# The opening of a two-layer backbone: modulation in quarters on four column tiles, the values of five row pairs summed side by side, in a hand-written order

## The chip, the cores and the metric

The kernel runs on one core of a Trainium2 chip, in one launch. Its engines are TensorE (PE in the profile, with its weight loads as PEld), VectorE (DVE), ScalarE (ACT), GpSimd (POOL) and SyncE (SP), which here does nothing but issue transfers. SBUF is the on-chip memory, PSUM the eight banks into which TensorE sums (128 partitions, 512 fp32 numbers per partition and bank). The metric is the device time of one execution in microseconds, the median over several runs.

## What is computed

A backbone of two layers over 1024 latent tokens and 256 context tokens of width 1024. Layer 0 is windowed attention with sink logits, layer 1 latent attention. The change touches only what comes first in layer 0: the modulation of the normalised tokens, and the projection onto the values.

```python
def adaln(cond, w, bias):
    m = jax.nn.silu(cond) @ w + bias
    return jnp.split(m, 3, axis=-1)          # shift, scale, gate

shift_x, scale_x, gate_x = adaln(c, ada_w[i], ada_b[i])
shift_c, scale_c, gate_c = adaln(c_ctx, ada_w[i], ada_b[i])
hx = rms_norm(x, norm_g[i]) * (1.0 + scale_x[:, None]) + shift_x[:, None]
hc = rms_norm(ctx, norm_g[i]) * (1.0 + scale_c) + shift_c
...
q, k, v, g = jnp.split(h @ w_in, [A_WIDTH, A_WIDTH + A_KV_WIDTH, A_WIDTH + 2 * A_KV_WIDTH], axis=-1)
```

Here `ada_w[0]` is 1024 x 3072 in fp32; its first 2048 columns (shift and scale) are 8 MB. The value columns of `w_in` are 256 wide.

## The kernel before, in words

**Tiling.** The 1280 tokens are ten row tiles of 128, in five pairs `p`: pair 0 is the context, pairs 1 to 4 the latent tokens. The width of 1024 is eight blocks `k` of 128 columns, taken in four quarters `b` of two blocks. A group is one pair and one quarter; there are 20.

**The opening** is everything until the first projection of the loop `proj_t`. For each row tile it loads the tile (`x_load`), sums its squares on ACT (`norm`, L692), takes the root on POOL (L693, L694) and scales the tile in place (`scale`, L701 on DVE, L699 on ACT). For each group it turns four 128 x 128 blocks on TensorE into a PSUM bank (`turn`, L712), multiplies and adds the modulation's columns on DVE (`h_part`, two instructions at L723), and cuts the result into a high part, rounded on ACT (L724), and the low remainder, a subtraction on POOL or DVE (`h_low`, L729). `v_part` then sums the values: for two blocks and two row tiles three matmuls each, high x high, low x high and high x low (`mm3`, L126, L127, L128), so 12 matmuls of 128 x 256 for each group. After a pair's fourth quarter ACT and DVE take the values out of PSUM (L745, L747).

**The modulation.** The columns of shift and scale come from `ada_mm`: the 1024 rows of `ada_w` pass as moving data in eight pieces `k`, with two columns of conditioning (latent, context) as weights, in two halves `h` of 512 shift and 512 scale columns. The shift's two rows land in PSUM partitions 0 and 1, the scale's in 32 and 33, of bank 6. `ada_cols` copies them out on ACT (L679), turns them into columns on TensorE (L681), and `set_cols` adds bias and gain on DVE (L168, L171). No `h_part` of quarters 0 and 1 can start before half 0 is complete, none of quarters 2 and 3 before half 1.

**Buffers.** `arena_f` holds staging in fp32: six pieces of `ada_w`, four row tiles, two pieces of the value weights and four group buffers. With four places for row tiles, pairs 0 and 1 run through all their quarters first, half 0 and then half 1, and pairs 2 to 4 follow. Four PSUM banks take the turned groups, two the values of a pair in turn.

**What sets the order.** In the opening the order on each engine is found by the scheduler of the language from the program's order and its own reckoning of readiness. From the loop on (`in_order = tc.manual_schedule()`) the program's order stands. All loads of the opening are issued by SP, which works through them in order; a load waits for the buffer it overwrites, and also for the transfer issued eight before it among all queues, since eight semaphores tell of landings in turn. Queues of the other engines are worked through in order as well.

**After the opening** come the projections of the first layer (ten column blocks of `w_in`, blocks 1 to 9 in the loop), with a vector computation of the remaining modulation beside them on DVE (`ada_vec`, L342 and L344).

## Time and profile before

| | us |
|---|---|
| median of 3 runs (1560.34 to 1561.45) | 1561.43 |
| the profiled execution, its own time | 1563.35 |
| its span, first to last instruction | 1561.6 |
| PE busy in the span | 1513.9 |
| DVE, ACT, POOL busy | 953.2, 714.1, 816.3 |
| HBM read and written | 131.13 MB, 46.15 MB |

The profiled execution's own time lies 1.75 us above its span, and 1.9 us above the median. In the page each line of the span in slices gives ten per cent steps of busy time for 40 equal slices of 39 us; the opening fills a little more than the first two of them, where PE reads 6 and 8 while it reads 9 nearly everywhere else.

### The profile page before, as it was taken

How to read it: one execution, taken by the hardware profiler on the slowest of the kernel's cores; microseconds unless marked ns; L12 is line 12 of the kernel's file. 1: busy time of each engine (PE TensorE's matmuls, PEld its weight loads, DVE VectorE, ACT ScalarE, POOL GpSimd, SP SyncE). 2: the span in 40 equal slices, each digit the busy share in tenths (PEclk: the TensorE clock that was granted, in tenths of full speed). 3: DMA queues.
4: the chain of work that ended last, by engine and by line, in shares of the span. 5: the costliest groups of instructions: out<-in, count | busy, mean ns of one | idle time of the engine just before them, and what ended most of it. 6: DMA issues, size and time to landing. Idle time of an engine off the chain costs nothing.

```text
span 1561.6 us, 24793 instructions
## 1 busy us (share of the span) xinstructions
PE 1513.9 (97%) x9074; PEld 1207.1 (77%) x9074; DVE 953.2 (61%) x1859; ACT 714.1 (46%) x1369; POOL 816.3 (52%) x764
## 2 busy tenths in 40 slices
PE   6899999999999999998999999999999999999998
PEld 2797888687888888887988788766876875885686
DVE  2666968827767787777826301556566566566644
ACT  2512212219877777776623332244443443453422
POOL 2652545417544443344517351278789789699200
PEclk8899999999999999999999999999999999999999
DMA  8425544474433322326304851402122112211442
GB/s 303 178 92 186 198 140 169 151 223 138 121 109 99 97 89 88 95 68 203 109 9 138 295 155 63 124 9 58 45 68 65 51 46 74 58 44 45 142 155 81
DMA packets 123986, 178.91 MB, mean 115 GB/s; under 512 B 11724, under 2 KB 72268, under 8 KB 123864
## 3 DMA queue, kind: packets, MB, share of 16 engines
q1 hardware_dynamic: 119032, 170.27, 34.8%
q10 hardware_dynamic: 4832, 7.06, 1.3%
q8 instruction: 71, 1.16, 0.3%
q14 instruction: 51, 0.42, 0.1%
HBM read 131.13 MB, written 46.15 MB: 114 GB/s over the span
## 4 chain that ended last, share of the span: by engine, by line
PE 86%; DMA 3%; DVE 3%; ACT 3%; issue 2%; POOL 2%; SPq 0%; POOLq 0%; DVEq 0%; ACTq 0%
PE PB L126 14%; PE PB L127 14%; PE PB L128 14%; PE PB L1345 12%; PE PB L1368 9%; PE PB L572 5%; PE PB L1311 5%; PE PB L562 4%; PE PB L532 2%; PE PB L533 2%; DMA arena_f<-a_w_in 1%; PE PB L1379 1%; DVE arena_f L344 1%; DMA arena_f<-b_w_in 1%; PE PB L355 1%
## 5 line engine op out<-in xcount | busy, mean ns | idle before, releaser
L126 PE MATMUL PB<-arena_r 128*128 128x512 f32 (+2 forms) x1312 | 477.2, 364 | 4.9 <-ACT arena_r L205 2.1
L127 PE MATMUL PB<-arena_r 128*128 128x512 f32 (+2 forms) x1312 | 470.0, 358 | 2.9 <-POOL arena_r L729 2.0
L128 PE MATMUL PB<-arena_r 128*128 128x512 f32 (+2 forms) x1312 | 469.8, 358 | 0.2 <-DVE arena_r L122 0.2
L126 PEld LDWEIGHTS PB<-arena_r 128*128 128x128 f32 x1312 | 250.6, 191 | 58.9 <-issue 16.0
L1361 POOL TENSOR_TENSOR arena_f<-arena_f 128x1024 f32<-128x1024 f32 x120 | 285.9, 2382 | 8.2
L127 PEld LDWEIGHTS PB<-arena_r 128*128 128x128 f32 x1312 | 250.4, 191 | 37.3 <-POOL arena_r L729 2.6
L128 PEld LDWEIGHTS PB<-arena_r 128*128 128x128 f32 x1312 | 250.2, 191 | 35.6 <-DVE arena_r L122 0.4
L1345 PE MATMUL PB<-arena_r 64*128 64x512 f32 (+1 forms) x1600 | 225.8, 395 | 0.0
L122 POOL TENSOR_TENSOR arena_r<-arena_f,arena_r 128x512 fp32r<-128x512 f32 x98 | 134.7, 1388 | 164.4 <-ACT arena_r L121 164.3
L1317 DVE TENSOR_REDUCE krF<-PB 128x1 f32<-128x512 f32 (+1 forms) x264 | 167.3, 678 | 79.6 <-PE PB L1311 79.6
L1355 ACT ACTIVATE arena_f<-PB 128x1024 f32<-128x1024 f32 x160 | 164.5, 1028 | 111.4 <-PE PB L1345 84.6
L122 DVE TENSOR_TENSOR arena_r<-PB,arena_r 128x512 fp32r<-128x512 f32 (+2 forms) x215 | 140.4, 664 | 92.4 <-ACT arena_r L121 91.5
L1345 PEld LDWEIGHTS PB<-arena_r 64*128 64x128 f32 (+1 forms) x1600 | 174.0, 185 | 17.2 <-issue 5.2
L121 ACT CAST arena_r<-PB 128x512 fp32r<-128x512 f32 (+2 forms) x215 | 120.4, 565 | 120.6 <-PE PB L128 74.0
L539 DVE CUSTOM_DVE_ANT_0 arena_f<-PB,arena_f,small 128x256 f32<-128x256 f32 (+1 forms) x288 | 145.4, 524 | 46.1 <-PE PB L533 39.4
L1368 PE MATMUL PB<-arena_f 128*64 128x512 f32 x640 | 145.9, 595 | 0.0
L545 ACT ACTIVATE arena_f<-arena_f,small 128x640 f32<-128x640 f32 (+2 forms) x160 | 118.9, 744 | 28.8 <-DVE small L539 27.9
L572 PE MATMUL PB<-arena_r 128*128 128x512 f32 x336 | 120.7, 435 | 4.2 <-ACT arena_f L583 4.1
L344 DVE SCALAR_TENSOR_TENSOR arena_f<-arena_f,small 128x512 f32<-128x512 f32 x98 | 112.9, 1198 | 11.6 <-DMA arena_f<-ada_w 11.3
L1311 PE MATMUL PB<-arena_r 64*128 64x512 f32 (+1 forms) x768 | 109.5, 354 | 0.7 <-DVE arena_r L122 0.7
L1368 PEld LDWEIGHTS PB<-arena_f 128*64 128x64 f32 x640 | 44.0, 137 | 79.6 <-issue 79.0
L562 PE MATMUL PB<-ident,arena_f 128*128 128x128 f32 x672 | 104.8, 273 | 0.5 <-ACT arena_f L545 0.3
(165 smaller groups left out, 1869.6 us busy)
## 6 DMA issues: line engine op xcount, KB each, us to landing
arena_r<-q_d SPq DMA_DIRECT2D x160, 128.0 KB, 3.0
arena_f<-ada_w SPq DMA_DIRECT2D x64, 256.0 KB, 3.6
arena_f<-a_w_in SPq DMA_DIRECT2D x40, 256.0 KB, 3.8
arena_f<-ada_w SPq DMA_DIRECT2D x16, 512.0 KB, 5.0
arena_f<-x SPq DMA_DIRECT2D x16, 512.0 KB, 6.3
q_d<-arena_f SPq DMA_DIRECT2D x16, 512.0 KB, 2.6
qn_d<-arena_f SPq DMA_DIRECT2D x16, 512.0 KB, 5.1
arena_r<-qn_d SPq DMA_DIRECT2D x16, 512.0 KB
```

Source lines behind the costliest of these rows:

```text
L122: (lo_eng or nc.vector).tensor_sub(lo, src, hi.bitcast(F32))
L126: nc.tensor.matmul(o, ah, bh, start=first, stop=False)
L127: nc.tensor.matmul(o, al, bh, start=False, stop=False)
L128: nc.tensor.matmul(o, ah, bl, start=False, stop=last)
L562: nc.tensor.transpose(pt[:, h, :], self.Ps[h][:, ci * 128 : ci * 128 + 128], ident)
L572: nc.tensor.matmul(self.pv, V[:, self.chunks[ci], self.g, :], PT[:, s], start=ci == 0 and s == 0, stop=ci == self.m - 1 and s == 1,)
L1311: nc.tensor.matmul(bank[:, o : o + n], self.q[r, s, bs], k[r, 0, n0 : n0 + n], start=s == 0, stop=s == 2)
L1317: nc.vector.reduce_max(self.mxp[:, e, b : b + 1, i], bank[:, 0:n], AX.X)
L1345: nc.tensor.matmul(PB[:, b + e, :], k[r, s, cs], q[r, sq], start=i == 0, stop=i == 4)
L1355: nc.scalar.activation(E, PB[:, b : b + 2, :], AF.Exp)
L1361: eng.tensor_add(acc, acc, E)
L1368: nc.tensor.matmul(PB[r, 7, :], Vq[:, c, h, :], E[:, e], start=c == 0, stop=c == NT - 1)
```

## The change

The opening is written anew, and its order is now the program's (a second `manual_schedule`).

- **Modulation in quarters.** `ada_load(q, kk)` loads two blocks of rows and 256 shift and 256 scale columns, in two transfers of 256 KB (32 transfers in place of 16 of 512 KB). `ada_mm(q, kk)` issues four matmuls of 256 columns into PSUM partitions 0, 32, 64 and 96: the even and the odd block are summed apart. `ada_cols` adds the two while it turns them, by a matmul with a selecting matrix `sel`. Each quarter of the modulation releases one quarter of the groups. The number of columns that pass through TensorE is the same.
- **All row tiles stay.** Ten places for row tiles, each with an address of its own; `ada_w` has four staging places.
- **Values of all pairs in five banks.** Bank `p` sums pair `p` over all quarters, so the groups can run quarter by quarter. That leaves banks 5 and 7 for turned groups (two in place of four) and two group buffers in place of four.
- **Order of a group's matmuls.** `v_part` issues its eight matmuls with the high part first, and then the four with the low part.
- **Smaller moves.** The mean and epsilon step goes from POOL to DVE for a pair at once, the root for a pair in one instruction; squares are written to PSUM or to `V` as scratch; three of the high parts and one weight cut are rounded on POOL.

```diff
+    awr = Ring(F, [0, 10, 14, 18], 1024)
+    hr = Ring(F, [62, 64], 512)
...
+    def ada_load(q, kk):
+        aw[q, kk] = shp(awr.next(), 2, 2, 256)
+        src = t["ada_w"][0, kk * 256 : kk * 256 + 256, 0 : 2 * D].rearrange("(k p) (a c) -> p k a c", p=128, a=2)
         for a in range(2):
-            nc.tensor.matmul(PA[32 * a : 32 * a + 2], sc[:, k, :], aw[h, k][:, a, :], start=k == 0, stop=k == 7)
+            load(out=aw[q, kk][:, :, a], in_=src[:, :, a, q * 256 : q * 256 + 256])
+
+    def ada_mm(q, kk):
+        for k in range(2):
+            for a in range(2):
+                r = 64 * k + 32 * a
+                nc.tensor.matmul(
+                    PA[r : r + 2, 0:256], sc[:, 2 * kk + k, :], aw[q, kk][:, k, a], start=kk == 0, stop=kk == 3
+                )
+
+    def ada_cols(q):
+        for j in range(2):
+            o = PA[:, 256 + 34 * j : 290 + 34 * j]
+            nc.tensor.matmul(o, am[0:98, j * 128 : j * 128 + 128], sel[0:98], start=True, stop=True)
...
+    def x_load(p):
+        xn[p] = [f_at(22 + 8 * p, 2, 1024), sm_ring(), sm_ring()]
...
+    def norm(p):
+        _, sq, st = xn[p]
+        nc.vector.tensor_scalar(st[:, 0:2], sq[:, 0:2], 1.0 / D, EPS, ALU.mult, ALU.add)
+        nc.gpsimd.tensor_tensor(st[:, 2:4], st[:, 0:2], mhalf.to_broadcast([128, 2]), ALU.pow)
...
             for k in (2 * b, 2 * b + 1):
-                mm3(o, [h[:, s, k, js] for s in range(2)], [W[:, s, k, :] for s in range(2)], k == j == 0, j == 1 and k == 7)
+                for s in range(2):
+                    nc.tensor.matmul(o, h[:, 0, k, js], W[:, s, k, :], start=k == j == s == 0, stop=False)
+        for j in range(2):
+            js = slice(j * 128, j * 128 + 128)
+            o = PB[:, p, j * 256 : j * 256 + 256]
+            for k in (2 * b, 2 * b + 1):
+                nc.tensor.matmul(o, h[:, 1, k, js], W[:, 0, k, :], start=False, stop=j == 1 and k == 7)
...
+    groups = [(p, q) for q in range(2) for p in range(3)] + [(3, 0), (3, 1), (4, 0), (4, 1)]
+    groups += [(p, q) for q in range(2, 4) for p in range(NP)]
+    NG = len(groups)
+
+    def make(i):
+        if i < NG:
+            turn(*groups[i], (5, 7)[i % 2])
+            h_part(*groups[i], nc.gpsimd.tensor_copy if i == 3 else nc.scalar.copy)
+        if i < 9:
+            h_low(*groups[i])
+        elif 10 < i <= NG:
+            h_low(*groups[i - 1], nc.vector if i % 2 or i in (14, 16) else nc.gpsimd)
+        if i == 9:
+            h_low(*groups[i])
+
+    opening = tc.manual_schedule()
+    opening.__enter__()
...
+    for i in range(3, NG):
+        p, q = groups[i]
+        if i > 7:
+            make(i + 2)
+        if i == 3:
+            scale(3, 0, nc.vector)
+            scale(3, 1, nc.scalar)
+        v_part(p, q)
+        if i < 8:
+            make(i + 2)
+        if i == 3:
+            square(4)
+            norm(4)
+        if i == 5:
+            scale(4, 0, nc.vector)
+            scale(4, 1, nc.scalar)
+            ada_mm(2, 0)
+            ada_mm(2, 1)
+            w0_cut(2)
+        if i == 6:
+            ada_mm(2, 2)
+            ada_mm(2, 3)
+            ada_copy()
+            w0_cut(3)
+        if i == 7:
+            ada_cols(2)
+            for kk in range(4):
+                ada_load(3, kk)
...
+        if i in (9, 11):
+            ada_mm(3, i - 9)
+            ada_mm(3, i - 8)
...
+        if i == 12:
+            ada_cols(3)
+        if i > 15:
+            v_out(p - 1)
...
+    v_out(4)
+    opening.__exit__(None, None, None)
```

**SP's queue from the program's start.** SP issues every load of the opening; L672 and L669 are pieces of `ada_w`, L688 and L694 row tiles, L753 and L761 pieces of the value weights. Before:

```order
L131 DMA small<-cc 128x16
L672 DMA arena_f<-ada_w 128x2x512 x3
L688 DMA arena_f<-ctx 128x1024 x2
L672 DMA arena_f<-ada_w 128x2x512
L753 DMA arena_f<-a_w_in 128x2x256 x2
L672 DMA arena_f<-ada_w 128x2x512 x4
```

Of the change:

```order
L131 DMA small<-cc 128x16
L694 DMA arena_f<-ctx 128x1024 x2
L669 DMA arena_f<-ada_w 128x2x256 x8
L761 DMA arena_f<-a_w_in 128x2x256
L694 DMA arena_f<-x 128x1024 x4
L761 DMA arena_f<-a_w_in 128x2x256
L669 DMA arena_f<-ada_w 128x2x256 x8
L694 DMA arena_f<-x 128x1024 x2
L761 DMA arena_f<-a_w_in 128x2x256 x2
L694 DMA arena_f<-x 128x1024 x2
L669 DMA arena_f<-ada_w 128x2x256 x16
```

The context's rows now go first. A first release of groups needs the eight small pieces behind them (2 MB) where it needed eight pieces of 512 KB (4 MB), of which four stand behind the context and the weights. The last row tiles go before half of the modulation; in the kernel before they were the last loads of the opening.

**PE's queue from the program's start.** L676 and L675 are the modulation's matmuls, L712 and L718 turn blocks, L681 and L685 make the modulation's columns, L126 to L128 and L742, L747 sum values. Before:

```order
L676 MATMUL PB<-arena_f,small 2x512 x6
L712 MATMUL PB<-ident,arena_f 128x128 x2
L676 MATMUL PB<-arena_f,small 2x512 x2
L712 MATMUL PB<-ident,arena_f 128x128 x6
L676 MATMUL PB<-arena_f,small 2x512 x8
L681 MATMUL PB<-ident,arena_f 128x34 x4
L712 MATMUL PB<-ident,arena_f 128x128 x4
L126 MATMUL PB<-arena_r 128x256
```

Of the change:

```order
L675 MATMUL PB<-arena_f,small 2x256 x12
L718 MATMUL PB<-ident,arena_f 128x128 x4
L675 MATMUL PB<-arena_f,small 2x256 x4
L685 MATMUL PB<-small,arena_f 128x34 x2
L742 MATMUL PB<-arena_r 128x256 x8
L747 MATMUL PB<-arena_r 128x256 x4
L718 MATMUL PB<-ident,arena_f 128x128 x4
L675 MATMUL PB<-arena_f,small 2x256 x8
L742 MATMUL PB<-arena_r 128x256 x8
```

The first value matmul stands behind one group's turns and a quarter of the modulation, where two groups' turns and a half stood before it. Pieces of the second quarter come between the value matmuls of the first groups.

**DVE's queue about a third of the way through the opening.** L723 and L726 make the group's product, L729 and L733 the low part, L701 and L711 scale a row tile, L703 is the mean and epsilon step that the change moved here. Before:

```order
L723 TENSOR_SCALAR arena_f<-PB,small 128x256 x4
L701 TENSOR_SCALAR arena_f<-arena_f,small 128x1024
L723 TENSOR_SCALAR arena_f<-PB,small 128x256 x6
L701 TENSOR_SCALAR arena_f<-arena_f,small 128x1024
L723 TENSOR_SCALAR arena_f<-PB,small 128x256 x3
```

Of the change:

```order
L733 TENSOR_TENSOR arena_r<-arena_f,arena_r 128x512
L703 TENSOR_SCALAR small<-small 128x2
L726 TENSOR_SCALAR arena_f<-PB,small 128x256 x2
L711 TENSOR_SCALAR arena_f<-arena_f,small 128x1024
L726 TENSOR_SCALAR arena_f<-PB,small 128x256 x2
L703 TENSOR_SCALAR small<-small 128x2
L726 TENSOR_SCALAR arena_f<-PB,small 128x256 x4
```

A step that waits for ACT's squares (L703) now stands between the products of two groups. Behind the opening all five queues hold the same instructions in the same order as before.

## The prediction

> **What bounds the kernel now.** I read the busy shares first, then stretches of the span, then the order of time on PE. The stretches split the span at 86.3 us, where the opening ends: the values of the last pair are taken out at 86.47, released by the last value matmul.

> ```profile
> core 0: us, PE busy (x) PEld busy (x) DVE busy (x) ACT busy (x) POOL busy (x), PEclk, DMA share, GB/s
> 0.00:86.30 86.30, 66.75 (x393) 46.31 (x394) 39.80 (x79) 34.34 (x63) 39.11 (x48) 0.88 0.62 218
> 86.30:1561.60 1475.30, 1447.13 (x8684) 1160.82 (x8682) 913.36 (x1780) 679.74 (x1306) 777.15 (x716) 0.99 0.35 109
> ```
> ```profile
> 86.47 0.65 ACT L745 CAST arena_r<-PB 128x256 fp32r<-128x256 f32 x2 [4.59 <-PE PB L128]
> ```

> Behind the opening PE is busy 98% of the time, and every queue there is unchanged, so what the opening gains or loses reaches the end as it is. Inside it PE lacks 19.6 us, and its clock was at half for part of the rest. Stretches cut where the clock changes show how (PEclk is the granted share):

> ```profile
> 17.57:20.98 3.41, 3.19 (x16) 0.45 (x12) 0.00 (x0) 0.00 (x0) 0.00 (x0) 1.00 1.07 385
> 20.98:24.40 3.42, 1.08 (x8) 0.57 (x7) 1.66 (x6) 3.02 (x6) 1.92 (x3) 1.00 1.04 390
> 24.40:31.20 6.80, 5.86 (x22) 3.52 (x21) 3.64 (x5) 2.03 (x4) 4.03 (x5) 0.50 1.05 386
> 44.88:48.29 3.41, 0.99 (x7) 0.46 (x5) 1.97 (x7) 3.08 (x6) 0.93 (x3) 1.00 0.98 344
> 48.29:55.10 6.81, 5.36 (x24) 5.07 (x25) 5.91 (x11) 5.09 (x9) 6.58 (x7) 0.50 0.40 158
> 55.10:68.78 13.68, 12.35 (x105) 12.14 (x104) 8.61 (x15) 7.75 (x16) 11.90 (x12) 1.00 0.63 215
> 68.78:72.19 3.41, 0.98 (x7) 0.79 (x8) 3.29 (x7) 2.37 (x5) 2.09 (x4) 1.00 0.15 56
> 72.19:75.60 3.41, 3.41 (x19) 3.41 (x18) 2.11 (x6) 0.97 (x3) 1.17 (x1) 0.50 0.00 0
> ```

> Three times PE has about 1 us of work in 3.4 us, and each time half clock follows. On PE the places are the first loads, the two turns of the modulation into columns, and the wait for the last row tiles:

> ```profile
> 5.64 5.26 PE L676 MATMUL PB<-arena_f,small 128*2 128x512 f32 x12 [5.64 <-DMA arena_f<-ada_w]
> 24.81 0.58 PE L126 MATMUL PB<-arena_r 128*128 128x256 f32 x1
> 27.14 0.41 PE L127 MATMUL PB<-arena_r 128*128 128x256 f32 x1
> 27.35 0.41 PE L128 MATMUL PB<-arena_r 128*128 128x256 f32 x1
> 47.74 0.33 PE L712 MATMUL PB<-ident,arena_f 128*128 128x128 f32 x1 [1.49 <-DVE arena_f L723]
> 57.94 0.60 PE L712 MATMUL PB<-ident,arena_f 128*128 128x128 f32 x4
> 58.29 0.36 PE L126 MATMUL PB<-arena_r 128*128 128x256 f32 x1
> 59.81 0.60 PE L712 MATMUL PB<-ident,arena_f 128*128 128x128 f32 x4
> 71.54 0.55 PE L712 MATMUL PB<-ident,arena_f 128*128 128x128 f32 x3 [2.28 <-ACT arena_f L699]
> 74.27 1.05 PE L712 MATMUL PB<-ident,arena_f 128*128 128x128 f32 x4
> 74.97 0.56 PE L126 MATMUL PB<-arena_r 128*128 128x256 f32 x1
> ```

> **Durations.** From one turn to the next (57.94 to 59.81) a group costs 1.87 us at full clock: turn 0.36, twelve matmuls 1.51. At half clock they cost 0.70 (74.27 to 74.97) and 12 x 0.21 = 2.5. The other engines, and the modulation in a warm stretch:

> ```profile
> L729 POOL TENSOR_TENSOR arena_r<-arena_f,arena_r 128x512 fp32r<-128x512 f32 x16 | 21.8, 1374 | 10.7 <-ACT arena_r L724 10.6
> L723 DVE TENSOR_SCALAR arena_f<-PB,small 128x256 f32<-128x256 f32 x40 | 19.8, 537 | 6.6 <-PE PB L712 5.2 <-POOL arena_r L729 1.2
> L724 ACT CAST arena_r<-arena_f 128x512 fp32r<-128x512 f32 x20 | 12.2, 617 | 13.7 <-DVE arena_f L723 13.5
> L692 ACT ACTIVATE arena_f<-arena_f 128x1024 bf16<-128x1024 f32 x10 | 10.6, 1056 | 17.8 <-DMA arena_f<-x 9.7 <-DMA arena_f<-ctx 8.0
> L701 DVE TENSOR_SCALAR arena_f<-arena_f,small 128x1024 f32<-128x1024 f32 x8 | 8.9, 1115 | 13.6 <-POOL small L694 13.6
> L729 DVE TENSOR_TENSOR arena_r<-arena_f,arena_r 128x512 fp32r<-128x512 f32 x4 | 3.5, 868 | 0.7 <-ACT arena_r L724 0.7
> L679 ACT COPY arena_f<-PB 34x512 f32<-34x512 f32 x2 | 1.2, 577 | 3.4 <-PE PB L676 3.4
> L681 PE MATMUL PB<-ident,arena_f 34*128 34x34 f32 x8 | 0.9, 231 | 1.5 <-ACT arena_f L679 1.5
> ```
> ```profile
> L676 PE MATMUL PB<-arena_f,small 128*2 128x512 f32 x4 | 1.0, 592 | 0.0
> ```
> ```profile
> L640 POOL CAST arena_r<-arena_f 128x512 fp32r<-128x512 f32 x8 | 4.7, 614 | 0.3 <-PE PB L127 0.3
> ```

> In the warm stretch the four records of one `ada_mm` would take 2.4 us one after the other and take 1.0: its two tiles run side by side. Four tiles of half the columns should take half of that, about 0.53 with the fill; two by two they would take 1.0 as now. I take 0.53, since nothing in the row tells partitions 64 and 96 from 0 and 32. [...]

> **Stage A, to the sum of the second quarter.** Here the loads decide. SP issues, up to the last piece of it, 2 context tiles, 16 modulation pieces, 2 weight pieces and 4 row tiles: 24 transfers, 7.86 MB. The first 0.52 MB landed at 5.64, and the rate over the rows from 17.57 to 31.20 is 385 to 390 GB/s: 5.64 + 7.34 / 0.385 = 24.7, and 25.0 with a little for smaller runs of bytes. The same sum gives 12.5 for the first quarter. Behind that: its last sum 0.86 at half clock, copy 0.58, two columns 0.46, bias and gain 0.5, two products 1.0, rounding on POOL 0.61, hand-offs 0.5: first value matmul at 17.0 instead of 24.81. The second group waits for pieces of the second quarter in PE's own queue (landed 22.4): it starts at 23.3 and ends at 25.8; a turn and two sums at half clock follow (0.70 + 2 x 0.86): 28.3. A bound below is 25.5, if the clock is full by then.

> **Stage B, eight groups, to the first half of the fourth quarter's sum.** Work on PE: 8 x 1.87, one turn 0.36, six sums 3.2, two pairs of columns 0.9: 19.4. Stalls, chain against cover:
> - the turn of the modulation into columns, 0.58 behind one turn of 0.36: 0.3;
> - the next group waits for bias and gain, two products and a POOL rounding (2.3) behind 1.87: 0.5;
> - pairs 1 and 2 in the second quarter: DVE makes a low part (0.87) or scales a tile (1.1) ahead of the products, then 1.0 and 0.62: 0.6 each, and 0.5 each for a low part on POOL (1.37) behind eight matmuls (about 1.0): 2.2;
> - pair 3: DVE's mean step stands ahead of its products and waits for two squares on ACT (2 x 1.06 and their sums): 1.1, its low part 0.4;
> - pair 4's scaling: 0.3.

> Together 4.8; none (0) if DVE and POOL keep ahead, up to 9 if POOL, with 14 us of work here, runs late. Stage B ends at 28.3 + 19.4 + 4.8 = 52.5. The loads hide: by the rate above the third quarter has landed by 38, ahead of its sums; the fourth is asked for as its buffers come free, from 39 on, and is needed from 50 on.

> **Stage C, ten groups.** A turn is now two groups ahead, so the chain of products 1.0, rounding 0.62 and low part 0.87 or 1.37 has 1.51 + 0.36 + 1.51 in front of it and is hidden. 10 x 1.87 - 2 x 0.36 (two turns fewer) + 2 x 0.53 + 0.46 = 19.5. The opening ends at 72.0.

> Sum: 72.0 - 86.3 = -14.3. The span becomes 1547.3, the profiled execution's own 1563.35 becomes 1549.1, and the median, 1.9 us lower, **1547.1**. Moving the mean step to DVE, the roots in one instruction, and rounding on POOL lie inside these chains. If the cover of the loads were gone, stage B would begin at the third quarter's landing, which adds up to 6.

> **Rivals.**
> - *The tiles run two by two.* Eight sums of stages B and C and one in A cost 0.43 more: 3.9, 1551.0. Against it stands nothing but that only two are seen.
> - *The clock falls again.* About 1 us of work in 3.4 was enough three times; stage B is 75% busy on average, but its stalls come in pairs. Each fall costs up to 3.4 (6.8 us at half). Two falls: 1553.9. [...]
> - *The gain is given back behind the opening.* The second block's weights and the first pieces of the later modulation must be ready 14 us sooner. They come behind 38 to 48 us of loads; DMA is at 0.15 and 0.00 from 68.78 on now, so there is room. Wholly given back: 1561.4.
> - *Slower: two banks and two group buffers in place of four make the groups serial.* Then each costs turn 0.6, products 1.0, rounding 0.62, low part 1.37, the last four matmuls 0.48 and hand-offs 0.4: 4.5, and 18 groups with the six-and-two sums and columns end at 28.3 + 81 + 6 = 115: 1590. It decides from (86.3 - 28.3 - 6) / 18 = 2.9 us a group on. Against it: turns go two groups ahead, and a bank is free again after turn and products, 1.6, while two groups take 3.7. Half way between the two, at 3.7 a group, it gives 1576.
> - *Better:* no stalls in B and half clock ended sooner in A: 7 less, 1540.

> **How the numbers follow.** Forecast with its own range 1541 to 1551: 0.58; tiles two by two 0.09; clock and longer stalls, 1551 to 1557: 0.16; better than 1541: 0.06; given back: 0.05; serial: 0.06. The range 1541 to 1556 leaves out the better side, the serial case, the gain given back and the tail of the stalls: some 2 in 10. A measurement of this kernel tells about 0.2% (3 us) from no change. Faster by more: 0.89; within: 0.05; slower: 0.06.

> **What would show it.** First value matmul near 17 us, the opening's last one near 72; no PE gap over 1.2 us after 28; the modulation's records in fours, about 0.5 us a piece; nothing changed between the opening's end and the end of the program (1475 us). I am wrong if half clock returns after 30 us, if the first value matmul is later than 20, if stage C costs over 2 us a group, or if PE waits for weights in the first projections.

## The result, and the profile after

The changed kernel takes 1544.83 us (median of 4 runs, 1543.46 to 1545.73) against 1561.39 for the kernel before on the same chip (1560.34 to 1561.45): 16.6 us less, a ratio of 0.9895 with a 95% interval of 0.9878 to 0.9912. Forecast were 1547.1 us, with a range of 1541 to 1556.

The stretches of the span after, cut where the clock changes and where the prediction's stages end (columns as in the prediction: length, busy time of PE, its weight loads, DVE, ACT, POOL, granted clock, DMA share, GB/s):

```profile
core 0: us, PE busy (x) PEld busy (x) DVE busy (x) ACT busy (x) POOL busy (x), PEclk, DMA share, GB/s
0.00:14.86 14.86, 6.28 (x32) 1.41 (x36) 2.51 (x11) 4.01 (x7) 1.11 (x6) 1.00 0.86 281
14.86:18.27 3.41, 1.07 (x12) 0.52 (x4) 1.39 (x5) 2.55 (x5) 1.87 (x3) 1.00 1.02 410
18.27:21.68 3.41, 2.94 (x13) 2.94 (x14) 2.48 (x5) 2.42 (x5) 1.70 (x3) 0.50 1.09 354
21.68:27.23 5.55, 5.24 (x53) 2.85 (x52) 3.22 (x6) 2.18 (x3) 1.87 (x2) 1.00 1.09 372
27.23:50.06 22.83, 21.33 (x193) 17.52 (x189) 13.99 (x32) 13.54 (x23) 13.05 (x12) 1.00 0.90 296
50.06:69.64 19.58, 19.58 (x177) 18.70 (x173) 14.36 (x29) 9.65 (x21) 10.52 (x8) 1.00 0.49 155
69.64:1543.10 1473.46, 1447.01 (x8683) 1163.33 (x8681) 917.82 (x1789) 680.55 (x1307) 776.19 (x716) 1.00 0.35 109
```

The opening ends at 69.64 where it ended at 86.30: 16.7 us, as much as the median's difference. (Five matmuls of the next projection already stand ahead of its last four; the cut at 69.64 leaves the same work behind it as the one at 86.30.) In the first stretch the 1.00 under PEclk says nothing, because the trace's record of the granted clock begins at 14.86. The turns at 13.52 below take 1.12 us where they take 0.60 later at full clock and took 1.05 at half clock in the kernel before (74.27), so PE ran at about half clock there. From 14.86 on, half clock is left in one stretch of 3.41 us, behind a stretch with 1.07 us of work. The last stage has no idle PE at all.

In each of the fourteen traces of this case all changes of the granted clock lie whole multiples of 3.41 us apart (before at 14.16, 17.57 and 24.40 us, after at 18.27 and 21.68), and where this grid lies differs from trace to trace. The clock is read below in stretches of that grid. The order of time on PE shows the seams (start, length, instruction, and in brackets the idle time before it and who ended it):

```profile
7.41 1.01 PE L675 MATMUL PB<-arena_f,small 128*2 128x256 f32 x2 [7.41 <-DMA arena_f<-ada_w]
9.59 4.00 PE L675 MATMUL PB<-arena_f,small 128*2 128x256 f32 x22 [1.17 <-DMA arena_f<-ada_w]
13.52 1.12 PE L718 MATMUL PB<-ident,arena_f 128*128 128x128 f32 x4
14.56 0.73 PE L675 MATMUL PB<-arena_f,small 128*2 128x256 f32 x8
15.82 0.63 PE L685 MATMUL PB<-small,arena_f 98*128 98x34 f32 x4 [0.53 <-ACT arena_f L680]
18.75 2.08 PE L742 MATMUL PB<-arena_r 128*128 128x256 f32 x8 [2.29 <-POOL arena_r L728]
21.48 0.71 PE L718 MATMUL PB<-ident,arena_f 128*128 128x128 f32 x4
26.25 1.04 PE L675 MATMUL PB<-arena_f,small 128*2 128x256 f32 x16
27.23 0.66 PE L718 MATMUL PB<-ident,arena_f 128*128 128x128 f32 x4
28.34 0.63 PE L685 MATMUL PB<-small,arena_f 98*128 98x34 f32 x4 [0.45 <-ACT arena_f L680]
31.27 1.21 PE L742 MATMUL PB<-arena_r 128*128 128x256 f32 x8 [0.35 <-POOL arena_r L728]
40.55 0.74 PE L747 MATMUL PB<-arena_r 128*128 128x256 f32 x4 [0.15 <-POOL arena_r L733]
59.12 0.60 PE L718 MATMUL PB<-ident,arena_f 128*128 128x128 f32 x4
60.99 0.60 PE L718 MATMUL PB<-ident,arena_f 128*128 128x128 f32 x4
69.67 0.74 PE L747 MATMUL PB<-arena_r 128*128 128x256 f32 x4
```

The value matmuls begin at 18.75 in place of 24.81, so 6.1 us of the gain lie ahead of them and 10.6 behind. Two pieces of the modulation (sixteen records) pass in 0.98 us, from 26.25 to 27.23, which is 0.49 a piece where two tiles take 0.92 (below): all four run side by side. From 59.12 to 60.99 a group costs 1.87, as before. The wait for the last row tiles (1.49 and 2.28 us in the kernel before) is gone.

Behind the opening the traces differ by up to 2 us without a cause in the change. Both have stretches at half clock, 3.41 us or twice that long, and their places differ: before at 311 and, twice as long, at 741; after at 848 and, twice as long, at 721. In the twelve kernels below the rest of the program took 1471 to 1474 us. That is why small effects are read from the opening's end as well as from the times.

### The profile page after: what moved, and what is told of

Same layout as the page of the kernel before. It is cut to its first block, busy times and chain, and to the rows that moved or that the text cites. A ratio compares the mean times of both kernels' runs of the same rounds, so it can differ in the third digit from the quotient of the medians.

```text
span 1543.1 us, 24967 instructions
## 1 busy us (share of the span) xinstructions
PE 1503.4 (97%) x9146; PEld 1207.3 (78%) x9146; DVE 955.8 (62%) x1875; ACT 714.9 (46%) x1369; POOL 806.3 (52%) x747
## 4 chain that ended last, share of the span: by engine, by line
PE 86%; DVE 3%; DMA 3%; POOL 3%; ACT 2%; issue 2%; POOLq 0%; SPq 0%; DVEq 0%; ACTq 0%
PE PB L126 14%; PE PB L128 13%; PE PB L127 13%; PE PB L1373 12%; PE PB L1396 9%; PE PB L573 5%; PE PB L1339 5%; PE PB L563 4%; PE PB L533 2%; PE PB L534 2%; DMA arena_f<-ada_w 1%; PE PB L1407 1%; PE PB L742 1%; DVE arena_f L345 1%; DMA arena_f<-b_w_in 1%
## 5 line engine op out<-in xcount | busy, mean ns | idle before, releaser
L126 PE MATMUL PB<-arena_r 128*128 128x512 f32 (+2 forms) x1232 | 451.5, 367 | 4.7 <-ACT arena_r L206 2.1
L127 PE MATMUL PB<-arena_r 128*128 128x512 f32 (+2 forms) x1232 | 445.5, 362 | 0.9 <-POOL arena_r L122 0.9
L128 PE MATMUL PB<-arena_r 128*128 128x512 f32 (+2 forms) x1232 | 445.7, 362 | 0.2 <-DVE arena_r L122 0.2
L126 PEld LDWEIGHTS PB<-arena_r 128*128 128x128 f32 x1232 | 233.3, 189 | 56.8 <-issue 14.3
L128 PEld LDWEIGHTS PB<-arena_r 128*128 128x128 f32 x1232 | 233.1, 189 | 35.6 <-DVE arena_r L122 0.4
L127 PEld LDWEIGHTS PB<-arena_r 128*128 128x128 f32 x1232 | 233.4, 190 | 34.2 <-POOL arena_r L122 1.6
L345 DVE SCALAR_TENSOR_TENSOR arena_f<-arena_f,small 128x512 f32<-128x512 f32 x98 | 113.3, 1201 | 13.5 <-DMA arena_f<-ada_w 13.2
```

The costliest lines, as they stand in the source:

```text
L126: nc.tensor.matmul(o, ah, bh, start=first, stop=False)
L127: nc.tensor.matmul(o, al, bh, start=False, stop=False)
L128: nc.tensor.matmul(o, ah, bl, start=False, stop=last)
```

## The experiments

The table gives for each kernel the median, its ratio to the kernel before with the interval, and the start of ACT's step that takes the last pair's values out. Five matmuls of the first projection (0.12 us each) already stand ahead of that step in the changed kernel and in its variants, twelve in the one with the old order of matmuls, eleven in the one with the late sink, none in the variant with the scheduler's order, in the kernel before and in its variants. The last column takes them off. The runs come from several chips, on which the kernel before took 1560.63 to 1561.76 us; each ratio is taken on one chip, a difference of medians may not be.

| kernel | median us | ratio, 95% | last pair out | less projection |
|---|---|---|---|---|
| before | 1561.39 | | 86.47 | 86.5 |
| changed | 1544.83 | 0.9895, 0.9878 to 0.9912 | 70.44 | 69.8 |
| two tiles | 1546.74 | 0.9911, 0.9898 to 0.9925 | 73.66 | 73.1 |
| low part between | 1549.49 | 0.9926, 0.9912 to 0.9941 | 74.44 | 73.0 |
| one bank | 1548.61 | 0.9925, 0.9909 to 0.9940 | 74.34 | 73.7 |
| scheduler's order | 1553.62 | 0.9957, 0.9943 to 0.9971 | 79.49 | 79.5 |
| sink late | 1543.54 | 0.9889, 0.9874 to 0.9904 | 73.31 | 72.0 |
| one more load | 1545.75 | 0.9906, 0.9890 to 0.9922 | 71.99 | 71.4 |
| before, low part last | 1557.09 | 0.9974, 0.9965 to 0.9983 | 82.82 | 82.8 |
| before, four tiles | 1553.34 | 0.9948, 0.9934 to 0.9962 | 78.61 | 78.6 |
| before, both | 1553.49 | 0.9949, 0.9935 to 0.9962 | 79.20 | 79.2 |
| warm | 1544.12 | 0.9890, 0.9877 to 0.9904 | 70.17 | 69.6 |
| three moved | 1543.20 | 0.9887, 0.9873 to 0.9900 | 69.34 | 68.7 |
| three moved, cut early | 1543.61 | 0.9884, 0.9867 to 0.9900 | 69.00 | 68.4 |

### Two tiles

```diff
-                r = 64 * k + 32 * a
+                r = 32 * a
                 nc.tensor.matmul(
-                    PA[r : r + 2, 0:256], sc[:, 2 * kk + k, :], aw[q, kk][:, k, a], start=kk == 0, stop=kk == 3
+                    PA[r : r + 2, 0:256], sc[:, 2 * kk + k, :], aw[q, kk][:, k, a],
+                    start=kk == k == 0, stop=kk == 3 and k == 1,
                 )
```

> The modulation's matmuls go to two column tiles (partitions 0 and 32) in place of four; nothing else is changed. Theory (four tiles really run at once, and a piece of the modulation is on PE's path): a pair of pieces takes about 2.0 us on PE where it took 1.04, and of the nine pieces that follow the first quarter's landing each costs 0.4 to 0.5 more, less some 0.5 that fills gaps: the opening ends 3 to 4 us later, about 1548.5. Rival (the pieces fill time in which PE waits for loads or for the other engines): the opening ends less than 1 us later, 1545 to 1546.

The rows of two pieces in the variant:

```profile
26.51 1.90 PE L675 MATMUL PB<-arena_f,small 128*2 128x256 f32 x16
28.34 0.66 PE L719 MATMUL PB<-ident,arena_f 128*128 128x128 f32 x4
```

The same sixteen records take 1.83 us where they took 0.98, so a piece costs 0.92 against 0.49. The stages end 1.1 us later in A (28.34 against 27.23), another 1.3 in B and 0.8 in C: 3.2 us at the opening's end, as the theory had it. The median is only 1.9 us higher (2.5 by the ratios), below the 1548.5 that was expected; in the profiled execution the rest was 1.4 us shorter than the changed kernel's. Four tiles do run at once, and they are on the path.

### Low part between

```diff
             for k in (2 * b, 2 * b + 1):
-                for s in range(2):
-                    nc.tensor.matmul(o, h[:, 0, k, js], W[:, s, k, :], start=k == j == s == 0, stop=False)
+                mm3(o, [h[:, s, k, js] for s in range(2)], [W[:, s, k, :] for s in range(2)], k == j == 0, j == 1 and k == 7)
-        for j in range(2):
...
-                nc.tensor.matmul(o, h[:, 1, k, js], W[:, 0, k, :], start=False, stop=j == 1 and k == 7)
```

> The twelve matmuls of a group go back to the old order, high x high, low x high, high x low for each block, so that the low part is needed at the group's second matmul and not at its ninth; nothing else is changed. Theory (in the first ten groups the high part is just in time and the low part comes 0.7 us behind it from DVE or 1.3 from POOL; later groups have two groups of cover): seven groups of the first ten wait 0.5 to 1.0 us more, 4 to 5 us together, and none of the last ten: about 1549. Rival (PE has enough to do ahead of each group): within 1 us of the changed kernel, 1545 to 1546.

The group of the low x high matmuls in the variant's opening (busy, mean ns, and behind the second bar the idle time of PE ahead of them):

```profile
L127 PE MATMUL PB<-arena_r 128*128 128x256 f32 x85 | 25.5, 300 | 3.4 <-POOL arena_r L733 2.5 <-DVE arena_r L733 0.9
```

PE waits 3.4 us for low parts, where the changed kernel waits 0.3 at L747; six waits of 0.2 to 0.8 us between 18 and 51 us make up nearly all of it. The opening ends 3.2 us later, where 4 to 5 were expected: the theory's mechanism with a smaller size. The last ten groups lose 0.5 of it, where nothing was expected. The median is 4.7 us higher; the profiled execution is the fastest of the four, 2.9 us below it.

### One bank

```diff
-            turn(*groups[i], (5, 7)[i % 2])
+            turn(*groups[i], 5)
```

Both single turns into bank 7 ahead of the loop go to bank 5 too. There the turn of pair 1's second quarter overwrites that of the context's before it is read, so the context's group is computed from the wrong block.

> All groups are turned in one PSUM bank in place of two by turns; nothing else is changed. Theory (a turn is issued one group ahead of its use in the first part and two groups ahead in the last ten, and the bank is free again after turn and two products, 1.6 us, while a group takes 1.87): no cost in the last ten groups, up to 0.3 us for each of some six groups before: 1545 to 1547. Rival (the groups are serial through the banks, the case of the prediction that ended slower): each of 18 groups would cost 1 us or more, 1560 and above.

```profile
32.72 1.35 PE L742 MATMUL PB<-arena_r 128*128 128x256 f32 x8 [1.76 <-POOL arena_r L728]
33.87 1.06 PE L747 MATMUL PB<-arena_r 128*128 128x256 f32 x4
```
```profile
30.23:33.65 3.42, 1.66 (x14) 1.42 (x13) 1.94 (x5) 0.32 (x2) 1.23 (x3) 1.00 1.05 377
33.65:37.06 3.41, 3.41 (x18) 3.41 (x17) 2.38 (x5) 1.88 (x3) 1.87 (x2) 0.50 1.11 349
```

Nothing is serial: the last ten groups still take 1.87 each, and the case of the prediction that ended slower falls. But the expected 0 to 2 us became 3.8. The product of the overwritten group has to wait for the turn that overwrites it, which leaves PE idle for 1.76 us, and the stretch around that has 1.66 us of work in 3.4: half clock follows for 3.4 us (33.65 to 37.06). Two later turns wait 1.19 and 0.79 for DVE to empty the bank. So the rival of the prediction "the clock falls again" is real in this place of the program. A single wait of 1.76 us was enough here (one of 1.74, with the late sink below, was not), and the changed kernel's longest in stage B are 0.45 and 0.35.

### The scheduler's order

```diff
-    opening = tc.manual_schedule()
-    opening.__enter__()
...
-    opening.__exit__(None, None, None)
```

> The same instructions and loads, but the order on each engine within the opening is again found by the scheduler, which lets the pieces of the modulation cut into the groups and takes three groups' turns ahead. Theory (the gain comes from quarters, resident row tiles and five sums, while the written order only saves part of the stalls): 2 to 5 us slower than the changed kernel, 1547 to 1550, so that most of the gain stays. Rival (the written order carries the gain): 1556 or more. Another: the written order does nothing, within 1 us.

```profile
20.82 0.33 PE L718 MATMUL PB<-ident,arena_f 128*128 128x128 f32 x1 [0.69 <-DVE arena_f L711]
23.12 0.60 PE L718 MATMUL PB<-ident,arena_f 128*128 128x128 f32 x3 [1.09 <-DVE arena_f L726]
25.74 0.48 PE L718 MATMUL PB<-ident,arena_f 128*128 128x128 f32 x1 [0.67 <-DVE arena_f L711]
```
```profile
16.66:20.08 3.42, 1.65 (x12) 1.49 (x12) 1.86 (x6) 3.15 (x5) 1.31 (x2) 1.00 1.03 394
20.08:23.49 3.41, 1.29 (x8) 0.76 (x7) 2.42 (x5) 2.25 (x6) 0.27 (x1) 1.00 1.10 351
23.49:30.32 6.83, 6.16 (x23) 2.69 (x22) 2.35 (x2) 1.38 (x2) 1.64 (x2) 0.50 1.07 378
```

8.8 us slower (9.7 by the ratios), between the theory (2 to 5) and its first rival (11 or more). At the opening's end structure alone brings 7.0 us of the 16.7, the written order the larger part. The first value matmul comes at 18.43, no later than in the changed kernel. Then the scheduler has turns of several groups ahead of the second group's matmuls on PE, and these turns wait for DVE to scale row tiles (L711) or to empty a bank (L726). Full clock outlasts a stretch with 1.65 us of work; the next has 1.29, half clock follows for 6.8 us, and the second quarter's sum ends at 35.3 where it ended at 27.23. Of the 9.7 us at the opening's end 8.1 stand there already.

### Sink late, and one more load

The sink logits are read far behind the opening only.

```diff
-        load2(out=nsink, in_=t["a_sink"].partition_broadcast(128))
-        nc.vector.tensor_scalar_mul(nsink, nsink, -1.0)
...
+        if i == 13:
+            load(out=nsink, in_=t["a_sink"].partition_broadcast(128))
+            nc.vector.tensor_scalar_mul(nsink, nsink, -1.0)
```

> The load of the sink logits, which lands at 9.36 us and for which DVE's first step after the constants waits until 9.39, and that step, are taken out of the start and come in the thirteenth group; nothing else is changed. Theory (up to the second quarter's sum the loads decide): the context's tiles are scaled 1 to 2 us earlier, the first value matmul may come up to 1 us earlier than 18.75, but the second quarter's last piece lands within 0.3 us of 26.49, its sum ends within 0.4 us of 27.23, and the opening ends within 0.4 us of where it does: 1544 to 1545. Rival (the chain from the first quarter to the first value matmul decides, PE has no slack behind it): everything comes 1 us or more earlier.

```diff
+    load(out=f_at(54, 1024), in_=src0(2))
     for kk in range(4):
         ada_load(1, kk)
```

> One more transfer of 0.52 MB, a row tile that nobody reads, stands in SP's queue ahead of the second quarter; nothing else is changed. Theory (the loads decide up to the second quarter's sum): its last piece lands 1.3 us later, at 27.8, the sum of it ends at 28.4 in place of 27.23, and the opening ends 1.0 to 1.5 us later, about 1546. Rival (PE or the first quarter's chain decides there): the sum ends within 0.3 us of 27.23 and the opening where it did.

With the late sink the first value matmul starts at 17.97, 0.78 earlier, and the second quarter's sum ends at 27.03, 0.2 earlier: the theory. The opening's end is 2.2 us later all the same (the median does not show it, since the rest of the program was 2.2 us shorter here), and that is the new place of the step: the theory's last part failed. DVE's negation waits in its queue for a load that SP issues behind others, with the low parts behind it:

```profile
62.14 0.17 DVE L861 TENSOR_SCALAR small<-small 128x16 f32<-128x16 f32 x1 [2.83 <-DMA small<-a_sink]
```
```profile
63.87 0.74 PE L745 MATMUL PB<-arena_r 128*128 128x256 f32 x4 [1.74 <-DVE arena_r L731]
```
```profile
61.62:65.03 3.41, 1.67 (x15) 1.47 (x14) 2.79 (x7) 1.22 (x3) 1.10 (x3) 1.00 0.48 152
65.03:68.44 3.41, 3.04 (x26) 2.84 (x25) 2.28 (x3) 1.53 (x4) 2.42 (x2) 1.00 0.44 139
```

The wait of 1.74 us leaves 1.67 us of work in its stretch, as much as the wait of 1.76 did with one bank, and here full clock stays.

With one more load of 0.52 MB the last piece of the second quarter lands at 27.72 in place of 26.49, and its sums run later:

```profile
27.87 1.04 PE L675 MATMUL PB<-arena_f,small 128*2 128x256 f32 x16
28.85 0.66 PE L718 MATMUL PB<-ident,arena_f 128*128 128x128 f32 x4
```

They end at 28.85, 1.6 us later, and the opening 1.6 us later. So a load more costs its full time, while 0.78 us less on the chain to the first value matmul brings 0.2: up to the second quarter's sum the loads decide, as the prediction had it. One thing blurs these two runs: half clock lasts 6.8 us here in both (17.24 to 24.07, 19.09 to 25.92) and 3.4 in the changed kernel. The run "warm" below is free of it.

### Two parts alone, on the kernel before

> The kernel before with one part of the change alone: the twelve matmuls of a group in the new order, the four with the low part last. Theory (the order hides the low part only where a high part is just in time): the two waits of PE for a low part on POOL at a half's first group (0.94 and 1.09 us in the kernel before) go, the other 17 us of idle PE stay: 1 to 2 us faster, 1559 to 1560. Rival (the order is most of the gain): 1552 or less. Another: nothing, since the next wait takes its place, 1561.

The edit is that of `v_part`, with bank `4 + p % 2`.

```profile
48.29:55.10 6.81, 6.80 (x58) 6.60 (x57) 4.52 (x11) 4.55 (x10) 6.13 (x7) 1.00 0.02 5
```

4.4 us faster, 3.7 at the opening's end, where 1 to 2 were expected. Both waits for a low part are gone, 2.0 us. The stretch of 6.81 us that ran at half clock before runs at full clock, but the wait that went is not what had brought its half clock: in the kernel before the clock fell at 48.29, and PE's wait for the low part came after that, up to 50.43. What brought it was the stretch from 44.88 to 48.29, in which the modulation's columns left PE 0.99 us of work. Here PE has the same waits behind the columns (1.49 and 0.58 us), 2.5 us earlier, and they lie across a boundary of the grid:

```profile
41.19:44.60 3.41, 1.89 (x12) 0.51 (x8) 0.75 (x5) 1.84 (x4) 0.16 (x1) 1.00 1.00 362
44.60:48.02 3.42, 2.04 (x14) 1.58 (x14) 3.42 (x8) 3.30 (x7) 2.90 (x6) 1.00 1.06 401
```

With 1.89 and 2.04 us of work in the two stretches full clock stays. That is luck of this one execution, which is also the fastest of the ten. The earlier half clock at 24 us lasts 3.4 us in place of 6.8, without the wait of 0.94 that stood in it. A later one comes at 65 to 72 us, around the wait for the row tiles, twice as long as before. How much of what exceeds the two waits is due to the order stays open.

```diff
+        for c in range(2):
+            for a in range(2):
+                r = 64 * c + 32 * a
+                nc.tensor.matmul(
+                    PA[r : r + 2, 0:256], sc[:, k, :], aw[h, k][:, a, 256 * c : 256 * c + 256], start=k == 0, stop=k == 7
+                )
-        for a in range(2):
-            nc.tensor.matmul(PA[32 * a : 32 * a + 2], sc[:, k, :], aw[h, k][:, a, :], start=k == 0, stop=k == 7)
```

> The kernel before with another part alone: the modulation's matmuls on four column tiles (shift and scale of two blocks of 256 columns each), halves and order of work as before. Theory (the first half's sums wait for loads anyway; the second half's eight pieces, 0.92 us each in a stretch where PE is busy, become 0.46): the second half's columns are done 2 to 4 us earlier than 45.81, and of that 1 to 3 us reach the opening's end, because the last row tiles set the end there: 1558.5 to 1560.5. Rival (four tiles are the main gain): 1555 or less. Another: nothing reaches the end, 1561.

```profile
41.96 0.39 PE L686 MATMUL PB<-ident,arena_f 98*128 98x98 f32 x2 [0.52 <-ACT arena_f L684]
64.81 0.55 PE L718 MATMUL PB<-ident,arena_f 128*128 128x128 f32 x3 [0.72 <-ACT arena_f L705]
```

8.2 us faster, and the theory's 1 to 3 fail. The first half of it held: the second half's columns come at 41.96 in place of 45.81, 3.9 us earlier. But I took the last row tiles for a fixed end, and they are not: they wait for places, and places come free as the groups run. So they came earlier too (SP asks for them at 54.09 in place of 59.74), PE's wait for them fell from 3.8 us to 0.7, and the half clock behind it (72.19 to 75.60) went.

> The kernel before with both parts that were tried alone (low parts last: 4.4 us faster; four column tiles: 8.2 us faster), and nothing else of the change: halves, four places for row tiles and the scheduler's order stay. Theory (both parts are worth more than their own waits because a short wait less keeps the clock from falling, so that they partly count the same thing; the wait for the last row tiles, 3.8 us in the kernel before, stays): 1550 to 1553, 5 to 8 us behind the changed kernel. Rival (they add up): 1548 to 1549. Another (they are the whole change): 1545.

```profile
62.06 0.74 PE L752 MATMUL PB<-arena_r 128*128 128x256 f32 x4 [1.07 <-POOL arena_r L735]
64.47 0.90 PE L718 MATMUL PB<-ident,arena_f 128*128 128x128 f32 x3 [1.53 <-ACT arena_f L705]
```

Both together are worth no more than the four tiles alone: 0.9949 against 0.9948. The two waits at 62 and 64 us bring half clock from 64 to 67. Against the changed kernel 8.7 us are missing, just over the upper end of what the theory gave. At the opening's end it is 9.4 us: 7.4 are the start of the value matmuls (26.20 against 18.75), which wait here for a half of the modulation, and 2 lie behind.

### Warm, three moved, and the cut

```diff
     ada_cols(0)
+    for _ in range(18):
+        nc.tensor.transpose(PB[:, 7, 0:128], xn[0][0][:, 0, 0:128], ident)
```

> Eighteen matmuls of 128 x 128 that nobody reads are issued between the first quarter's columns and the first value matmul of the changed kernel, where PE waits 2.3 us; nothing else is changed. Theory (about 1 us of work in 3.4 us lets the clock fall, and the loads decide the end of the second quarter's sum): the half clock from 18.3 to 21.7 goes, the first group's twelve matmuls take 1.5 us in place of 2.7, PE then waits for the second quarter's pieces, and its sum ends at 26.9 to 27.2 as it does now: 1544.4 to 1545. Rival (PE's half clock is on the path): the sum and the opening end 1.2 us or more earlier.

```profile
13.16:16.58 3.42, 2.90 (x30) 2.15 (x28) 0.87 (x3) 1.09 (x2) 1.89 (x2) 1.00 1.04 408
16.58:19.99 3.41, 2.63 (x22) 2.26 (x19) 2.10 (x6) 3.02 (x7) 1.68 (x2) 1.00 1.05 377
19.99:23.40 3.41, 2.38 (x15) 0.72 (x14) 2.83 (x6) 1.50 (x4) 0.69 (x1) 1.00 1.11 349
```

With 2.4 to 2.9 us of work in the stretches of this trace's grid, where the changed kernel had one with 1.07, the clock stays full. The grid's place alone does not explain that: the changed kernel and its six variants above all have half clock here, this kernel and the two below, which keep the eighteen matmuls, have none. The first group's twelve matmuls run from 18.36 to 20.07 in place of 18.75 to 21.67, yet the second quarter's sum ends at 27.01, 0.2 us earlier, and the opening 0.3 us earlier. The half clock that was left costs next to nothing, because loads cover it.

```diff
     x_load(2)
-    w0_load(1)
...
     for kk in range(4):
         ada_load(1, kk)
+    w0_load(1)
...
-    w0_cut(1)
     for kk in range(2):
         ada_mm(1, kk)
...
     ada_copy()
+    w0_cut(1)
     turn(0, 1, 7)
...
                 ada_load(3, kk)
+            load(out=nsink, in_=t["a_sink"].partition_broadcast(128))
...
     v_out(4)
+    nc.vector.tensor_scalar_mul(nsink, nsink, -1.0)
```

> The changed kernel with three things moved: the eighteen matmuls that keep the clock up, the sink logits' load behind the last quarter's pieces and their negation at the opening's end, and the second piece of the value weights behind the second quarter (with its cut behind the second copy of the sums). Theory (loads and PE decide together, so that both must come earlier): the second quarter's last piece lands at 25.6, its sum ends at 26.0 to 26.4 in place of 27.23, and the opening ends 0.8 to 1.2 us earlier, 1543.6 to 1544.1. Rival (a wait in the next groups takes it back, at the weights' cut or at the first groups of the second quarter): the opening ends within 0.4 us of where it does.

The second quarter lands at 24.81, its sum ends at 25.64, 1.6 us earlier, and the opening 1.1 us earlier. Half a microsecond was taken back at the first group of the second quarter. First the steps of DVE there, then POOL's:

```profile
27.49 0.16 DVE L167 TENSOR_TENSOR small<-PB,small 128x4 f32<-128x4 f32 x1 [0.34 <-PE PB L683]
27.68 0.92 DVE L170 SCALAR_TENSOR_TENSOR small<-small 128x4 f32<-128x4 f32 x1
```
```profile
27.29 1.29 POOL L764 TENSOR_TENSOR arena_r<-arena_f,arena_r 128x512 fp32r<-128x512 f32 x1 [6.19 <-ACT arena_r L763]
```

A step of 4 numbers a row, 0.16 us elsewhere, took 0.92: it ended at 28.60, when POOL's subtraction ended (28.58). L167, which reads PSUM, had its 0.16 beside the same POOL step.

> The last kernel (three things moved) with the cut of the second weight piece back at its old place, ahead of the second quarter's sums in the program. Theory (0.75 us of its gain went to a DVE step of 0.16 us that took 0.92, from 27.68 until POOL's subtraction for that cut ended at 28.58): the subtraction runs from about 26.2 to 27.5, ahead of that step, the step takes 0.16 again, PE's wait at the first group of the second quarter falls from 1.10 to about 0.35, and the opening ends 0.5 to 0.8 us earlier than there, 1542.4 to 1542.8. Rival (the wait is POOL's own queue, or the cut on ACT delays the group ahead of it by as much): the opening ends where it does there or later.

```profile
26.66 1.34 DVE L731 TENSOR_TENSOR arena_r<-arena_f,arena_r 128x512 fp32r<-128x512 f32 x1 [0.99 <-ACT arena_r L726]
28.11 0.17 DVE L170 SCALAR_TENSOR_TENSOR small<-small 128x4 f32<-128x4 f32 x1
```
```profile
26.19 1.27 POOL L764 TENSOR_TENSOR arena_r<-arena_f,arena_r 128x512 fp32r<-128x512 f32 x1 [5.18 <-ACT arena_r L763]
```

The small step has its 0.17 again, but the long one ahead of it, 0.69 us in the kernel with three moved, now takes 1.34 (to 28.00) beside the subtraction that it meets (26.19 to 27.46). Both theories were half right: PE's wait fell from 1.10 to 0.57, and the opening ends 0.3 us earlier. This last kernel has the shortest opening, 1.4 us under the changed kernel's, but the times do not tell the two apart (0.9884, interval 0.9867 to 0.9900, against 0.9895, interval 0.9878 to 0.9912).

## Why the prediction was right, step by step

Its sum had the opening end at 72.0; it ended at 69.6. The mechanism stood in each stage, with these sizes:

- **First quarter landed**: forecast 12.5, by the trace 13.89. The term used the rate of the steady part, 385 GB/s, right after the first landing; from 5.64 to 9.36 us it was 267, from there to 14.86 it was 370. The sink logits, a transfer of 8 KB that landed only at 9.36, are part of it, since PE waits 1.17 us for pieces at 8.4 and SP waits 1.4 us for that transfer; with the late sink the first value matmul came 0.78 earlier. The same 1.4 to 1.8 us came back in the second quarter's landing (26.49 for 25.0) and in the first value matmul (18.75 for 17.0). The 0.3 us that the prediction put on smaller runs of bytes was the author's estimate, and no run isolates it.
- **End of stage A**: 28.3 forecast, 27.23 measured, though the loads were later. The step "a turn and two sums at half clock follow" failed: full clock was back at 21.68, so the turn and the two sums cost 0.53 and 0.98 in place of 0.70 and 1.72. The second group ended at 25.72, as forecast (25.8), but by luck: it started at 24.18 in place of 23.3, and its twelve matmuls, priced at half clock with 2.5, took 1.54 at full clock. That half clock lasted one stretch of the grid and not two is luck too: it lasted two in four of the variants. It is worth little, since the three of them without a further load end the stage at 27.03 to 27.70.
- **Stage B**: 24.2 forecast, 22.83 measured. Work was 19.4 in the sum, so stalls were 3.4 where 4.8 was taken. The columns (0.45 for 0.3) and the first group's chain (0.6 for 0.5) stood as priced. The largest term, 1.1 for pair 3 behind DVE's mean step, did not: DVE does idle 2.9 us there for ACT's squares, until 37.40, but two sums (1.0 us) and a turn stand on PE just then, and PE waited 0.16.
- **Stage C**: 19.5 forecast, 19.58 measured, with 1.87 a group and two turns ahead.
- **A piece of the modulation**: 0.53 forecast, 0.49 measured. That four tiles run at once was the author's estimate from the two that ran side by side before. Two tiles in place of four cost 3.2 us, where the rival had 3.9.
- **Behind the opening**: forecast no change, and the opening's 16.7 us against the median's 16.6 say the same. The profiled spans differ by 18.5, of which 1.8 lie in the rest, where the length changes by as much between kernels with identical queues.

Of the rivals, two tiles at a time and serial groups are excluded by their runs. The clock did not fall again in the opening of the changed kernel once it was full: the least work in a stretch there was 2.96 us (25.10 to 28.51). It did in two variants: after one wait of 1.76 us (1.66 us of work in the stretch), and after a few turns that waited 0.34 to 1.09 us each for DVE (1.29 us of work). The second is the kernel without the written order, whose gain at the opening's end was 7.0 us.

What stays open is how the 10.6 us behind the first value matmul divide between resident row tiles, five banks and the order. Four tiles and low parts last are worth 3 us each when undone, but on the kernel before 8 and 4, and together no more than 8.

## What to carry to other kernels

Price a stall of TensorE with what may follow it: waits of 1 to 2 us in these openings were at times followed by 3.4 to 6.8 us of half clock (3.4 after 1.76 us with one bank), and at times, with much the same wait, by none (1.74 us with the late sink). Parts tried alone were worth about twice what they removed themselves, and did not add up. So do not credit a part with a fall of the clock that one trace lacks before you have seen which stretch had brought it. Ask of each wait that a step names what else stands on the waiting engine at that moment: a load decides only while PE has nothing else, and a late engine costs nothing behind work that is queued ahead of it. A structural change that needs a tight order should be costed with the order written out, because here the scheduler's order gave more than half of the gain back.

## What the runs showed of the hardware

With three things moved, a DVE step with both inputs in SBUF took 0.92 us in place of 0.16 beside a POOL subtraction that reads SBUF, and with the cut early one took 1.34 in place of 0.69; they ended 0.02 and 0.55 us behind POOL's end, while a step with one input in PSUM kept its 0.16. The openings of the fourteen traces hold more of these meetings. A DVE subtraction of 128 x 512 that began while POOL was in one of that size ended 0.55 to 0.68 us behind POOL's end, 43 times out of 43 (in the kernel before it took 1.42 from 58.35 on, and POOL's ended at 59.23); the 91 others took 0.67 to 0.69. No run isolated the cause.
